# Two matrix products in the bilinear form: sums on one engine, joined and in pairs, in new orders

## The chip, the cores and the metric

The kernel runs on one core of a Trainium2 chip. The metric is device time in microseconds (us) of one execution. The engines are TensorE (PE, matrix products into the eight banks of PSUM; PEld is its weight load), VectorE (DVE), ScalarE (ACT), GpSimd (POOL), and SyncE (SP, which here only issues DMAs). Each engine works through its own instructions in order and waits for the others by semaphores.

## The reference, cut to what matters

```python
batch, m, k, h, n = 16, 512, 768, 3072, 768
y = np.matmul(x, w1) + b1          # x: 8192 rows of 768 in all, w1: 768 x 3072
y = np.maximum(y, 0)
return np.matmul(y, w2)            # w2: 3072 x 768
```

Inputs and result are float32. The kernel multiplies in float16 and collects sums of squares of its inputs (`stat`), by which a flag at the end chooses a general path, which is not taken here.

## The kernel before

**Blocks.** The hidden axis of 3072 is done in two halves (`c` = 0, 1), the 8192 rows in eight blocks of 1024 (`MB`). That makes 16 blocks of work, `it` = 0 to 15; blocks 0 to 7 are the first half, 8 to 15 the second. Block 8 has the rows of block 7 again, so x stays where it is across the switch, and new w1 and w2 are loaded there. The results of the second half are added in DRAM to those of the first by accumulating DMAs from GpSimd's queue; only the last block reads the earlier result back and adds it on the core (`add_priors`, `add_prior`).

**Stages.** A block has two stages, each a matrix product in a bilinear form of the kind of Strassen's, with 20 products of sub-blocks in place of 24. In the first stage (`add_first`, L878) x is a 4 x 2 grid of sub-blocks and w1 a 2 x 3 grid, for each of two groups of columns: 40 products of six matmuls (256 columns each), L896. In the second (`add_second`, L995) y is a 4 x 3 grid, w2 a 3 x 2 grid: 20 products of eight matmuls (384 columns each), L1016. Block 0's first stage is a plain product instead (L802).

**Sums.** A product multiplies a sum of x sub-blocks by a sum of w1 sub-blocks. `X_SUMS`, `Y_SUMS`, `W1_SUMS` and `W2_SUMS` list them as (output, input, input, sign): numbers below 8 for x (12 for y, 6 for w) are the sub-blocks as loaded, higher ones are sums. `FIRST_U`, `FIRST_V`, `SECOND_U` and `SECOND_V` say which sum a product takes. `place` (L202) gives each its slot; slots of dead sub-blocks are used again. A block needs 16 sums of x (L640, 768 elements a partition, five of them on GpSimd by `X_POOL`) and 16 of y (L869). A y sum covers both column groups (1024 elements) where `Y_JOIN` names it; the others are done for each group (512), six of these twelve on GpSimd by `Y_POOL`. The y sums of a block can be made when its first stage has given the y sub-blocks; the x sums of the next block when its x has been loaded (GpSimd's queue, L565) and transposed by eight DMAs on SP (L619). The sums of w1 (L657, for each group) and w2 (L679) are made in block 0 and at the switch, where the planner may put each on VectorE or GpSimd.

**Chains.** Products add up in PSUM along chains. `SECOND_CHAINS` lists them: ('m', p) is product p, ('t', t) is operation t of `SECOND_OPS`, which reads the chain's two banks and writes an output (`out`, to one of four buffers `o` and from there to DRAM), a kept sum (`sum`, in `s`) or the starting value of another chain (`seed`, into PSUM). An operation with a kept sum as second operand runs on VectorE (L1031), one without on ScalarE (L1028). A chain of the second stage holds two banks, one of the first stage one. `SECOND_ORDER` and `FIRST_ORDER` are the orders of TensorE's products; `SWITCH_ORDER` is that of blocks 7 and 8, `LAST_ORDER` that of block 15.

**The planner.** `Graph.run` is a list scheduler: each task has an engine, a cost in ns written in the code (a y sum of 1024: 685, one of 512: 426, on GpSimd 1180; an x sum: 552, on GpSimd 1650), a due time and an allowance for crossing to another engine (`CROSS`). TensorE's order is fixed; the planner sets the order on the other engines and gives out banks, kept-sum places and output buffers. The instructions are issued in that order. Its squares (`idle` tasks) fill gaps of ScalarE.

## Time and profile before

| what | value |
|---|---|
| median of 3 runs | 1073.01 us (1070.94 to 1074.68) |
| the profiled execution | 1072.51 us, span 1070.9 us |
| granted TensorE clock, mean | 0.951 |
| DMA | 115.15 MB, mean 108 GB/s |
| block 4: first stage, second stage | 26.20 us, 38.51 us |
| starts of the first stages, blocks 1, 7, 9, 15 | 78.36, 469.50, 615.26, 1002.59 us |

The lines below are of the profiled execution, in us from its span's start. A line of the timeline has start, length, engine, line of the kernel, operation, output<-input with shapes, count, and in brackets the idle time before it and what ended that. A line of the groups has count | busy us, mean ns of one | idle time before them and what ended most of it. A line of the windows has the stretch, its length, the busy time and count of each engine named in its header, TensorE's granted clock, the busy share of the DMA engines, and GB/s. For one source line, min/median/max of an instruction are given.

### The profile page before, as it was taken

To read this page: it belongs to the slowest core of one execution; us is meant where nothing else is said; L and a number is where in the kernel's file an instruction comes from. 1 tells how busy PE (TensorE), PEld (TensorE's weight loads), DVE (VectorE), ACT (ScalarE), POOL (GpSimd) and SP (SyncE) were. 2 spreads that over 40 slices of the span, in tenths; PEclk is the share of its full clock that TensorE was granted. 3 is DMA by queue.
4 is the path that set the end of the run, shared out by engine and by line. 5 is a ranking of instruction groups with operands and counts; after the bars stand their busy time and mean duration, and the time that the engine had idled before them with its cause. 6 is when DMAs were issued, how large, how long until landed. Compare 5 with 4: busy or idle time off the path is not lost. (4 is left out here: it accounts for less than half of the span.)

```text
span 1070.9 us, 16568 instructions
## 1 busy us (share of the span) xinstructions
PE 905.8 (85%) x6445; PEld 644.0 (60%) x6445; DVE 831.7 (78%) x1060; ACT 472.9 (44%) x919; POOL 440.5 (41%) x333
## 2 busy tenths in 40 slices
PE   9889798896978969788688896986979889797986
PEld 8458376483755738466356483763847658484763
DVE  4888959679696886958976879586796978869694
ACT  7737557563461725525324173463523415152340
POOL 6521605216052250615652617244272552716353
PEclk9999899898999999899889899999999999899998
DMA  9963283852638345183315572855738586461833
GB/s 210 174 160 73 47 188 52 172 109 53 169 52 185 60 97 133 45 184 107 115 74 89 80 123 40 143 89 89 109 53 142 81 135 103 68 111 30 120 117 119
DMA packets 159717, 115.15 MB, mean 108 GB/s; under 512 B 93052, under 2 KB 158100, under 8 KB 159380
## 3 DMA queue, kind: packets, MB, share of 16 engines
q0 software_dynamic: 46496, 54.27, 32.6%
q1 hardware_dynamic: 112672, 58.81, 22.4%
q8 instruction: 51, 0.84, 0.3%
q10 hardware_dynamic: 468, 1.00, 0.2%
q14 instruction: 30, 0.25, 0.1%
HBM read 73.94 MB, written 55.05 MB: 120 GB/s over the span
## 5 line engine op out<-in xcount | busy, mean ns | idle before, releaser
L1016 PE MATMUL ps<-v,y 128*128 128x384 f16 x2560 | 468.9, 344 | 142.8 <-DVE o L1031 51.9
L1016 PEld LDWEIGHTS <-y 128*128 128x128 f16 x2560 | 260.9, 102 | 347.2 <-issue 179.8
L896 PE MATMUL ps<-x,v 128*128 128x256 f16 x3600 | 399.9, 274 | 12.9 <-DVE s L936 4.3
L896 PEld LDWEIGHTS <-v 128*128 128x128 f16 x3600 | 353.6, 98 | 58.8 <-issue 15.7
L869 DVE TENSOR_TENSOR y<-y 128x1024 f16<-128x1024 f16 (+1 forms) x266 | 272.2, 1065 | 12.9 <-POOL y L869 9.7
L869 POOL TENSOR_TENSOR y<-y 128x512 f16<-128x512 f16 x96 | 134.9, 1422 | 341.5 <-ACT y L930 230.5
L933 DVE CUSTOM_DVE_ANT_0 y<-ps,s 128x512 f16<-128x512 f32 x240 | 161.9, 688 | 92.3 <-PE ps L896 54.5
L640 POOL TENSOR_TENSOR x<-x 128x768 f16<-128x768 f16 x70 | 133.7, 1918 | 85.3 <-DVE x L640 60.1
L1028 ACT ACTIVATE ps<-ps 128x768 f32<-128x768 f32 x80 | 63.6, 795 | 232.4 <-PE ps L1016 138.8
L930 ACT ACTIVATE s<-ps,bt 128x256 f32<-128x256 f32 x180 | 74.0, 471 | 180.8 <-PE ps L896 164.7
L640 DVE TENSOR_TENSOR x<-x 128x768 f16<-128x768 f16 x154 | 123.3, 847 | 2.1 <-DMA x<-xn 2.0
L1060 POOL DMA_DIRECT2D out_dram<-o x56 | 67.3, 1245 | 64.1 <-DVE o L1031 62.8
L930 ACT ACTIVATE y<-ps,bt 128x256 f16<-128x256 f32 x180 | 73.3, 471 | 29.2 <-PE ps L896 27.8
L1028 ACT ACTIVATE s<-ps 128x768 f32<-128x768 f32 x64 | 51.7, 808 | 75.3 <-PE ps L1016 73.2
L1031 DVE TENSOR_TENSOR o<-ps,s 128x768 f32<-128x768 f32 x60 | 57.1, 952 | 29.5 <-ACT ps L1028 19.8
L1031 DVE TENSOR_TENSOR o<-s,ps 128x768 f32<-128x768 f32 x60 | 56.6, 949 | 25.0 <-PE ps L1016 11.7
L565 POOL DMA_DIRECT2D xn<-in_x_dram x30 | 23.4, 782 | 97.7 <-DVE y L933 65.4
L627 ACT ACTIVATE xn<-xn 128x768 f16<-128x768 f16 x60 | 50.1, 839 | 1.6 <-DMA x<-xn 1.6
L926 ACT ACTIVATE ps<-ps 128x512 f32<-128x512 f32 x60 | 34.7, 582 | 24.1 <-DVE y L933 15.8
L930 ACT ACTIVATE ps<-ps,bt 128x256 f32<-128x256 f32 x60 | 26.9, 448 | 17.2 <-PE ps L896 11.5
L802 PE MATMUL ps<-x,v 128*128 128x256 f16 (+1 forms) x216 | 31.9, 308 | 0.8 <-DMA v<-in_w_dram 0.5
L679 DVE TENSOR_TENSOR v<-v 128x768 f16<-128x768 f16 x36 | 27.8, 808 | 3.9 <-DMA v<-in_w_dram 3.9
(65 smaller groups left out, 407.0 us busy)
## 6 DMA issues: line engine op xcount, KB each, us to landing
out_dram<-o SPq DMA_DIRECT2D x71, 384.0 KB, 6.2
xn<-in_x_dram POOLq DMA_DIRECT2D x28, 768.0 KB, 7.9
out_dram<-o POOLq DMA_DIRECT2D x56, 384.0 KB, 6.8
x<-out_dram SPq DMA_DIRECT2D x8, 384.0 KB, 3.4
v<-in_w_dram POOLq DMA_DIRECT2D x6, 384.0 KB, 8.8
v<-in_w_dram POOLq DMA_DIRECT2D x12, 192.0 KB, 10.1
w1d<-in_w_dram POOLq DMA_DIRECT2D x6, 384.0 KB, 17.2
w2d<-in_w_dram POOLq DMA_DIRECT2D x12, 192.0 KB, 15.1
```

What stands on the lines that cost most here:

```text
L627: self.nc.scalar.activation(out=self.xn[:, s, :], in_=self.xn[:, s, :], func=ACTF.Square, accum_out=self.stat[:, self.stat_at["x"] + i:][: ...
L640: e.tensor_tensor(out=x[:, a], in0=x[:, b], in1=x[:, c], op=ALU.add if sign > 0 else ALU.subtract)
L802: nc.tensor.matmul(self.ps[:, ps.at[0], cols], lhsT=self.v1[:, gi, 2 * h + k2, k, j * P:(j + 1) * P], rhs=rhs, start=(k2 == 0 and k == 0), ...
L869: e.tensor_tensor(out=self.y[:, a, cols], in0=self.y[:, b, cols], in1=self.y[:, c, cols], op=ALU.add if sign > 0 else ALU.subtract)
L896: nc.tensor.matmul(self.ps[:, at, j * self.QM:(j + 1) * self.QM], lhsT=self.v1[:, gi, self.w1s[FIRST_V[p]], k, j * P:(j + 1) * P], rhs=sel ...
L926: nc.scalar.activation(out=out, in_=ps, scale=float(a), func=func if kind == "out" else ACTF.Copy)
L930: nc.scalar.activation(out=out[:, halves[j]], in_=ps[:, halves[j]], func=func, scale=float(a), bias=beta(j))
L933: nc.vector._custom_dve(TENSOR_ADD_SAT, out=out, in0=ps, in1=s, s0=F_MAX, s1=0.0)
L1016: nc.tensor.matmul(self.ps[:, bank[ch].at[j], 0:NH], lhsT=self.y[:, self.ys[SECOND_U[p]], m0:m0 + P], rhs=self.v2[:, slot[SECOND_V[p]], s, :],
L1028: nc.scalar.activation(out=out, in_=ps, func=ACTF.Copy, scale=float(a))
L1031: engine.tensor_tensor(out=out, in0=in0, in1=in1, op=ALU.add if a == b else ALU.subtract)
L1060: nc.gpsimd.dma_start(out=rows, in_=out, accum_op=ALU.add)
```

## The change

All sums go to VectorE; GpSimd keeps its DMAs and the adds of the last block. A y sum always covers both column groups (1024 elements), except in block 0, and a w1 sum covers both groups (2 x 768). Where `X_FUSE` or `Y_FUSE` names a sum, it and the next one of the table become one operation over two slots each (`two`): as one run where the slots lie side by side, as two rows where not. A block has 10 + 3 operations for its x sums and 12 + 2 for its y sums. The tables of sums, the bilinear form of the second stage (seven chains in place of eight) and the orders of products in both stages are new; the order of blocks 7 and 8 is that of the others. In blocks 0 and 7 (`APART`) an output that has a kept sum as second operand leaves in two parts: SP stores the kept sum, ScalarE copies the banks to an output buffer, and GpSimd's accumulating DMA adds that in DRAM. The squares write to a tile of their own (`junk`) instead of an output buffer, in halves for w2, and are spread over more blocks (`STATS`). The planner's allowance from TensorE to others is 0.15 instead of 0.22 us, and tasks with a choice of two engines are gone.

```diff
-FIRST_ORDER = (16, 0, 36, 4, 12, 28, 8, 7, 18, 24, 9, 1, 15, 38, 21, 10, 3, 14, 35, 30, 6, 11, 32,
-    17, 37, 34, 5, 27, 31, 29, 2, 26, 22, 19, 25, 33, 20, 23, 39, 13)
-SWITCH_ORDER = (16, 4, 8, 0, 18, 15, 1, 10, 12, 14, 6, 17, 11, 7, 13, 9, 5, 2, 3, 19, 36, 24, 32,
-    28, 38, 29, 27, 35, 21, 30, 23, 34, 37, 31, 26, 20, 25, 22, 33, 39)
...
-Y_SUMS = ((13, 3, 4, 1), (18, 0, 13, 1), (14, 2, 8, 1), (15, 11, 5, 1), (12, 9, 10, 1), (27, 8, 7,
-    1), (19, 7, 14, 1), (16, 6, 12, 1), (20, 1, 19, 1), (17, 10, 15, 1), (21, 17, 3, -1), (23, 15,
-    16, 1), (22, 21, 0, -1), (25, 18, 20, 1), (26, 11, 10, 1), (24, 14, 16, -1))
-SECOND_U = (1, 19, 6, 4, 22, 12, 27, 0, 23, 13, 5, 16, 18, 7, 24, 26, 25, 2, 17, 10)
...
+FIRST_ORDER = (36, 4, 16, 20, 12, 0, 8, 7, 9, 18, 24, 28, 10, 1, 15, 3, 21, 38, 32, 14, 35, 29,
+    27, 30, 11, 34, 23, 26, 37, 31, 6, 5, 17, 25, 2, 22, 13, 33, 39, 19)
+SWITCH_ORDER = (36, 4, 16, 20, 12, 0, 8, 7, 9, 18, 24, 28, 10, 1, 15, 3, 21, 38, 32, 14, 35, 29,
...
+Y_SUMS = ((16, 3, 0, 1), (21, 5, 3, 1), (15, 8, 7, 1), (12, 11, 10, 1), (19, 5, 16, 1), (18, 1,
+    15, 1), (20, 2, 19, 1), (14, 6, 9, -1), (17, 11, 14, -1), (22, 1, 17, 1), (26, 18, 20, 1),
+    (24, 7, 22, 1), (13, 4, 12, -1), (23, 11, 9, 1), (27, 13, 14, 1), (25, 13, 16, -1))
+SECOND_U = (6, 2, 8, 26, 5, 21, 17, 23, 27, 19, 13, 4, 25, 12, 15, 11, 24, 18, 0, 1)
+SECOND_V = (0, 5, 7, 17, 9, 0, 10, 3, 16, 11, 14, 1, 13, 4, 1, 8, 12, 15, 3, 4)
...
 SECOND_OPS = {
...
+    0: (0, 1, 11, 1, 'out', 4, None),
+    1: (2, 1, 9, 1, 'out', 5, None),
+    2: (1, 1, 11, 1, 'out', 6, None),
+    3: (2, 1, None, None, 'out', 7, None),
+    4: (1, 1, 8, 1, 'out', 2, None),
+    5: (3, -1, 8, 1, 'out', 3, None),
+    6: (0, -1, 9, 1, 'out', 0, None),
+    7: (3, 1, None, None, 'out', 1, None),
+    8: (1, -1, 13, 1, 'sum', None, None),
+    9: (0, 1, 10, 1, 'sum', None, None),
+    10: (4, 1, 16, -1, 'sum', None, None),
+    11: (5, 1, None, None, 'sum', None, None),
+    12: (5, -1, None, None, 'seed', 0, None),
+    13: (6, 1, None, None, 'sum', None, None),
+    14: (5, 1, 16, 1, 'seed', 2, None),
+    15: (1, -1, None, None, 'seed', 5, None),
+    16: (1, 1, None, None, 'sum', None, None),
+    17: (3, -1, 19, 1, 'seed', 1, None),
+    18: (4, -1, None, None, 'seed', 3, None),
+    19: (6, 1, None, None, 'sum', None, None),
...
-SECOND_ORDER = (11, 17, 19, 1, 15, 5, 18, 13, 6, 14, 3, 2, 10, 12, 9, 0, 7, 16, 8, 4)
...
-X_POOL = (0, 2, 4, 12, 14)
-Y_POOL = ((0, 4), (0, 8), (0, 9), (0, 11), (1, 2), (1, 8))
-Y_JOIN = (0, 3, 5, 6, 7, 10, 12, 13, 14, 15)
+SECOND_CHAINS = ((('m', 2), ('t', 9), ('m', 14), ('t', 0), ('m', 3), ('t', 6)), (('m', 9), ('t',
+    16), ('m', 13), ('t', 15), ('m', 10), ('t', 8), ('m', 11), ('t', 4), ('m', 8), ('t', 2)),
+    (('m', 7), ('t', 3), ('m', 16), ('t', 1)), (('m', 1), ('t', 17), ('m', 18), ('t', 7), ('m',
+    12), ('t', 5)), (('m', 19), ('t', 18), ('m', 17), ('t', 10)), (('m', 15), ('t', 14), ('m', 6),
+    ('t', 12), ('m', 0), ('t', 11)), (('m', 5), ('t', 19), ('m', 4), ('t', 13)))
+SECOND_SEEDS = (12, 17, 14, 18, None, 15, None)
+SECOND_ORDER = (19, 5, 1, 4, 9, 17, 13, 18, 15, 10, 12, 6, 7, 11, 2, 0, 14, 8, 16, 3)
...
+X_FUSE = (3, 8, 11)
+Y_FUSE = (2, 13)
...
-    CROSS = {"PE": 0.22, "DVE": 0.08, "ACT": 0.08, "POOL": 0.1, "SP": 0.1}
+    CROSS = {"PE": 0.15, "DVE": 0.08, "ACT": 0.08, "POOL": 0.1, "SP": 0.1}
...
+APART = (0, 7)
+
+STATS = ((1, 2, 3, 4, 5, 6, 7), (2, 3, 4))
...
+    def sums_of(self, table, slots, fused):
+
+        n, out = 0, []
+        while n < len(table):
+            m = 2 if n in fused else 1
+            rows = [[slots[v] for v in table[n + k][:3]] for k in range(m)]
+            sign = table[n][3]
+            if m == 2:
+                rows = self.ordered(*rows, sign)
+            out.append((*(tuple(v) for v in zip(*rows)), sign))
+            n += m
+        return out
+
...
+    @staticmethod
+    def two(view, at):
+
+        if len(at) == 1:
+            return view[:, at[0]]
+        a, b = at
+        if a == b:
+            return view[:, a:a + 1].to_broadcast([P, 2, view.shape[2]])
+        return view[:, a:b + 1:b - a]
...
+        for out, in0, in1, sign in self.sums_of(X_SUMS, self.xs, X_FUSE):
+            def add(out=out, in0=in0, in1=in1, sign=sign):
                 x = self.x.rearrange("p a k m -> p a (k m)")
-                e.tensor_tensor(out=x[:, a], in0=x[:, b], in1=x[:, c],
-                                op=ALU.add if sign > 0 else ALU.subtract)
-            self.g.add(engine, 1650 if engine == "POOL" else 552, add,
-                       reads=[("x", q, h) for q in (b, c) for h in range(2)],
-                       writes=[("x", a, h) for h in range(2)])
+                self.nc.vector.tensor_tensor(
+                    out=self.two(x, out), in0=self.two(x, in0), in1=self.two(x, in1),
+                    op=ALU.add if sign > 0 else ALU.subtract)
+            self.g.add("DVE", 552 if len(out) == 1 else 950, add,
+                       reads=[("x", q, h) for q in in0 + in1 for h in range(2)],
+                       writes=[("x", a, h) for a in out for h in range(2)])
...
+    def add_w1_sums(self):
+
+        for o, i, j, sign in W1_SUMS:
             a, b, d = (self.w1s[q] for q in (o, i, j))
 
+            def add(a=a, b=b, d=d, sign=sign):
+                w = self.v1.rearrange("p g a k h -> p g a (k h)")
+                self.nc.vector.tensor_tensor(out=w[:, :, a], in0=w[:, :, b], in1=w[:, :, d],
+                                             op=ALU.add if sign > 0 else ALU.subtract)
+            self.g.add("DVE", 950, add,
+                       reads=[("w1", g, q) for g in range(2) for q in (b, d)],
+                       writes=[("w1", g, a) for g in range(2)])
...
-                self.g.add(engine, 685 if both else 1180 if engine == "POOL" else 426, add,
-                           reads=[k for q in (b, c) for h in gs for k in self.y_keys(q, h)],
-                           writes=[k for h in gs for k in self.y_keys(a, h)])
+    def add_y_sums(self, groups=(0, 1)):
+
+        n = len(groups)
+        cols = slice(512 * groups[0], 512 * groups[-1] + 512)
+        for out, in0, in1, sign in self.sums_of(Y_SUMS, self.ys, Y_FUSE if n == 2 else ()):
+            def add(out=out, in0=in0, in1=in1, sign=sign):
+                y = self.y[:, :, cols]
+                self.nc.vector.tensor_tensor(
+                    out=self.two(y, out), in0=self.two(y, in0), in1=self.two(y, in1),
+                    op=ALU.add if sign > 0 else ALU.subtract)
+            self.g.add("DVE", 426 if n == 1 else 685 if len(out) == 1 else 1217, add,
...
-                combine(nc.scalar if u is None else nc.vector, out, ps, a,
-                        None if u is None else sum_of(kept[u]), b)
-
-        def store(to, reg):
+                alone = u is None or (kind == "out" and apart)
+                combine(nc.scalar if alone else nc.vector, out, ps, a,
+                        None if alone else sum_of(kept[u]), b)
+
+        def store(to, reg, plain):
             out, rows = self.o[:, reg.at[0]].rearrange("p (a n) -> p a n", a=2), \
                 self.rows_of(it, to)
-            if c == 0 or final:
+            if plain:
                 nc.sync.dma_start(out=rows, in_=out)
             else:
                 nc.gpsimd.dma_start(out=rows, in_=out, accum_op=ALU.add)
+
+        def store_sum(to, u):
+            (nc.gpsimd if c else nc.sync).dma_start(
+                out=self.rows_of(it, to), in_=sum_of(kept[u]),
+                **({"accum_op": ALU.add} if c else {}))
...
+                elif u is not None and apart:
+                    assert b == 1
+                    self.g.add("POOL" if c else "SP", 1375 if c else 100,
+                               lambda to=to, u=u: store_sum(to, u), reads=[kept[u]],
+                               writes=[("out", self.block(it), to)], lat=6.5)
+                    engine = "ACT"
...
-                plain = c == 0 or final
+                plain = c == 0 and (u is None or not apart) or final
```

197 lines of the change are left out of this document (72 added, 125 removed), and 4 rows, old and new, of the table SECOND_CHAINS.

## The prediction, made before the result was known

> **What bounds the kernel now.** I read the busy shares first, then one block by stages, then the timelines of TensorE, VectorE and GpSimd over the same stage.
>
> ```profile
> PE 905.8 (85%) x6445; PEld 644.0 (60%) x6445; DVE 831.7 (78%) x1060; ACT 472.9 (44%) x919; POOL 440.5 (41%) x333
> ...
> core 0: us, PE busy (x) PEld busy (x) DVE busy (x) ACT busy (x) POOL busy (x), PEclk, DMA share, GB/s
> 340.36:366.56 26.20, 26.20 (x242) 23.49 (x241) 17.80 (x29) 16.73 (x39) 1.42 (x1) 1.00 0.45 113
> 366.56:405.07 38.51, 28.66 (x163) 16.09 (x161) 32.79 (x34) 11.82 (x21) 20.37 (x15) 0.96 0.50 103
> ```
>
> The first stage of a block is pure TensorE, 26.2 us at a clock of 1.00. The second takes 38.5, and VectorE is busy for 32.8 of it.
>
> ```profile
> 366.56 4.06 PE L1016 MATMUL ps<-v,y 128*128 128x384 f16 x24
> 371.12 1.47 PE L1016 MATMUL ps<-v,y 128*128 128x384 f16 x8 [0.50 <-DVE y L869]
> 373.54 6.66 PE L1016 MATMUL ps<-v,y 128*128 128x384 f16 x40 [0.94 <-ACT ps L1028]
> 384.95 5.74 PE L1016 MATMUL ps<-v,y 128*128 128x384 f16 x24 [4.76 <-ACT ps L1028]
> 392.42 4.06 PE L1016 MATMUL ps<-v,y 128*128 128x384 f16 x24 [1.72 <-DVE ps L1031]
> 397.36 2.76 PE L1016 MATMUL ps<-v,y 128*128 128x384 f16 x16 [0.88 <-ACT ps L1028]
> 401.17 4.06 PE L1016 MATMUL ps<-v,y 128*128 128x384 f16 x24 [1.05 <-DVE s L1031]
> ```
>
> Forty matmuls take 6.66 and eight 1.47, so 32 take 5.19: 0.162 each, 1.30 a product of eight, 26.0 for the 20 products. The other 12.5 us are the gaps in brackets (9.85), 1.68 of slow matmuls after the long gap (24 take 5.74, not 4.06), and some 0.17 of pipeline end at each gap. Why VectorE is late:
>
> ```profile
> 360.93 0.69 DVE L869 TENSOR_TENSOR y<-y 128x1024 f16<-128x1024 f16 x1
> 362.14 0.41 DVE L869 TENSOR_TENSOR y<-y 128x512 f16<-128x512 f16 x1
> 377.52 4.12 POOL L640 TENSOR_TENSOR x<-x 128x768 f16<-128x768 f16 x2
> 378.14 2.01 DVE L869 TENSOR_TENSOR y<-y 128x1024 f16<-128x1024 f16 x1
> 384.60 1.82 POOL L640 TENSOR_TENSOR x<-x 128x768 f16<-128x768 f16 x1 [2.96 <-DVE x L640]
> 384.85 1.99 DVE L640 TENSOR_TENSOR x<-x 128x768 f16<-128x768 f16 x1
> 389.69 1.56 POOL L565 DMA_DIRECT2D xn<-in_x_dram  x2
> 390.94 0.54 DVE L640 TENSOR_TENSOR x<-x 128x768 f16<-128x768 f16 x1
> ...
> 366.56:405.07 38.51, 15.41 (x12) 7.07 (x5) 0.96 0.50 103
> ...
> 366.56:405.07 38.51, 8.33 (x11) 9.86 (x5) 0.96 0.50 103
> ```
>
> A sum of 1024 takes 0.69 alone and 2.01 beside a GpSimd sum; one of 768 takes 0.54 beside a GpSimd DMA issue and 1.99 when it starts inside a GpSimd sum: it ends 0.4 after that sum. The last two rows are the window for the y line and the x line alone (VectorE, then GpSimd). Twelve y sums took 15.41; eight of 1024 and four of 512 at the free price are 7.2. Eleven x sums took 8.33, free 6.0. So 10.5 us a block are lost on VectorE to GpSimd's sums, nearly TensorE's idle time.
>
> **The change, part by part.** Prices:
>
> ```profile
> L869 DVE TENSOR_TENSOR y<-y 128x1024 f16<-128x1024 f16 x150 | 184.3, 1251 | 8.0 <-POOL y L869 5.2
> L640 DVE TENSOR_TENSOR x<-x 128x768 f16<-128x768 f16 x154 | 123.3, 847 | 2.1 <-DMA x<-xn 2.0
> L1063 POOL TENSOR_TENSOR x<-x,s 128x768 f32<-128x768 f32 x8 | 15.5, 1962 | 10.1 <-DVE s L1031 10.1
> L1031 DVE TENSOR_TENSOR o<-ps,s 128x768 f32<-128x768 f32 x60 | 57.1, 952 | 29.5 <-ACT ps L1028 19.8 <-PE ps L1016 4.9 <-DMA out_dram<-o 2.8
> L1028 ACT ACTIVATE ps<-ps 128x768 f32<-128x768 f32 x80 | 63.6, 795 | 232.4 <-PE ps L1016 138.8 <-DVE s L1031 55.7 <-DVE o L1031 22.1
> L619 SPq DMA_TRANSPOSE x<-xn x112: 1210/1275/3133, 40.3 to 966.8; - x112
> ...
> DMA to landing us min/median/max: 2.7/2.8/8.0
> ```
>
> *Sums.* No row shows a sum of two neighbours. From 512 to 1024 costs 0.28, so 2048 costs about 1.25 and 1536 about 0.97. A block's y sums become 12 at 0.69 and two at 1.25, 10.8; its x sums 10 at 0.54 and three at 0.97, 8.3. The rest of VectorE's block is 24.7: the two windows hold 17.80+32.79 = 50.6, less the second stage's sums (15.41+8.33) and the first stage's four y sums (two of 0.69, two of 0.41). Together 43.8, under TensorE's 26.2+26.0 = 52.2, although VectorE takes over all that GpSimd did (mean 1251 and 847 ns of VectorE's own sums fall to 690 and 540). The two-row form could instead run at half speed: one y and one x sum a block would grow by 1.12 and 0.84, each joined w1 sum by 0.84. I take full speed, as the rows are whole contiguous runs like those measured, and keep the other as a rival. The Trainium skill ("Vector Engine (DVE) Microarchitecture Reference", section 5.1, Performance modes) asks 16-bit operands and an innermost step of one for the fast mode, which two rows meet; no run here shows it yet. By that page the sum stands; without it the half-speed rival below would hold.
>
> *Orders.* I walked one steady block with the rows' times, 0.2 from the end of a product to its reader. A product can start when the operation before it in its chain has read or seeded its banks and its y sum is there; VectorE and ACT take their operations in the order in which the planner put them. Second stage, first product (19) at 0, one more each 1.30, as SECOND_ORDER has them. Product 1 is third, due at 2.60; its seed t18 reads product 19 on ACT behind the first stage's last output, 1.6 to 2.4: in time. Product 9, due at 5.20, needs t17, which waits for product 1 (3.9) and has VectorE from 4.1 to 5.05. Product 6, due at 14.3, needs t14: product 15 ends at 11.7, VectorE is free at 12.2, done 13.15. Product 11, due at 16.9, needs t8: 13.2 to 14.1. Product 14, due at 20.80, needs t9, done 20.80 to 20.85. Product 3, due at 24.75, needs t0: 22.3 to 23.3. Between them run the y sums (their order is the diff's): the fused pair 15 and 12 from 1.9 to 3.1, needed from 7.8; ten of the twelve behind the first stage are done by 9.0, the last two (20 and 26, needed at 24.75) by 11.3; then x sums between the outputs, to 21.9. So nothing waits over 0.1 us, and every product has another one between it and its seed; in the old order some follow their seed at once (the gaps of 0.88 to 1.05). The first stage walks through likewise, with 0.3 us to spare at the tightest (t0, before product 14). I charge 1.0 us a block for what a walk misses; the bounds are 0 and the three quoted gaps of about 1 plus one more, 3.8.
>
> *Transposes.* Three single x sums and one pair move into the first stage, on VectorE, behind six DMA transposes on SP. A first-stage product is 26.2/40 = 0.656; the raw places are last read by the 26th and the 30th product, free 17.1 and 19.7 us into the stage; at 1.3 each the sixth goes out at 21.0 and lands at 23.8, VectorE gets there at 24.2. This cover is thin: a landing of 8.0 instead of 2.8 makes VectorE 4.8 late, with the last two outputs and the y sums queued behind, of which products 1 and 9 have 1.3 to spare. At the median it costs 0.
>
> *GpSimd and SP.* GpSimd keeps x loads and accumulating stores; its queue only gets emptier, and loads go out earlier. Output buffers: four, each held until its store lands.
>
> ```profile
> L1060 POOL DMA_DIRECT2D out_dram<-o x56: 1179/1197/1651, 603.1 to 1006.2; - x56
> ...
> L1058 SPq DMA_DIRECT2D out_dram<-o x71: 372/372/414, 59.9 to 1064.2; - x71
> ```
>
> In blocks 0 and 7, six outputs go to ACT (0.80, it is busy 11.8 of 38.5) instead of VectorE (0.95), with six plain stores on SP (0.37) and six accumulating ones on GpSimd (1.2) more, 12 transfers of 384 KB in all. Each accumulating store waits on GpSimd for its plain store's landing, with the next x and w loads queued behind it, of which the first is needed a block later; nothing of TensorE waits for them, but the kept sums hold their places until their store lands. A gain is there too: six times 0.95 off VectorE. Between a loss of 6 us (one landing) and that gain, per block; I take the gain into VectorE's sums below and 1 us of loss into the two items below. The rearranged squares stay on ACT: 0.
>
> ```profile
> 19.87 22.91 PE L802 MATMUL ps<-x,v 128*128 128x256 f16 x138 [0.35 <-DVE x L752]
> 45.34 2.93 PE L1016 MATMUL ps<-v,y 128*128 128x384 f16 x16 [2.57 <-DVE v L679]
> 78.36 26.36 PE L896 MATMUL ps<-x,v 128*128 128x256 f16 x240 [0.61 <-DVE o L1031]
> 469.50 2.78 PE L896 MATMUL ps<-x,v 128*128 128x256 f16 x24
> 615.26 26.56 PE L896 MATMUL ps<-x,v 128*128 128x256 f16 x240
> 1002.59 26.36 PE L896 MATMUL ps<-x,v 128*128 128x256 f16 x240
> 1028.79 11.86 PE L1016 MATMUL ps<-v,y 128*128 128x384 f16 x72
> 1062.37 2.75 DVE L1031 TENSOR_TENSOR o<-x,ps 128x768 f32<-128x768 f32 x4
> ```
>
> *The sum.* Twelve steady blocks (1 to 6, 9 to 14) took (469.50-78.36)+(1002.59-615.26) = 778.5; now 12 x (52.2+1.0) = 638.4. Blocks 7 and 8 took 145.8; VectorE gets two blocks of 43.8 less 8.3 (no x sums between, the same rows follow), less 5.7 (outputs on ACT), plus 12 w1 sums of 0.97 and 24 w2 sums of 0.54 (22 of all these were GpSimd's), 98 of 104.4. The new order of block 8 draws on both groups of w1 from the start, so all 12 w1 sums must be done with block 7: 11.6, 8.7 of y sums and five operations of 0.95 are 25.1 of its 26.0. Tight, so I take 2 us lost in each block, 108.4; the bounds are 0 and the 10 us that the w1 sums would be late if their loads came last. Block 0 ended at 78.36. Its opening run ends at 42.8 and the second stage began at 45.34 behind a w2 sum; its first two products now need two plain w2 blocks and y sums of that moment, 43.3, it lasts 26.0, and I give 3.7 for the sums of w that trail into block 1: 73. The bounds are 69.3 and 78.4. The last block took 68.3. Its second stage, walked with six GpSimd adds of 1.96, the last four in a row from 22.4, has VectorE done after 31.3 instead of 1062.37+2.75-1028.79 = 36.3: 63.2. Span 73+638.4+108.4+63.2 = 883. The profiled execution was 1072.5 for a span of 1070.9, 0.5 under the median of 1073.0: 883+1.6+0.5 = 885.
>
> **Rivals.** *Half-hidden chains:* three or four gaps of about 1 us stay in each second stage, since they come from product-to-seed latency and not from sums. For: the rows 0.94, 0.88, 1.05. Against: the new order puts a product between. 14 blocks x 2.8 more: 924. *Transfers:* the same bytes in 0.83 of the time raise the DMA share from about 0.5 to 0.6 and more; landings near the maxima (8.0) hold the transposes or the four output buffers, 2 us a block: 913. *Half-speed pairs:* 2 us of VectorE in each of 14 blocks, half of it seen since VectorE has 8 us to spare, and 12 x 0.84 = 10 us in each of two runs of w1 sums, 18 of 20 seen: 917. *The other side:* the inflated sums are VectorE's own price, from something that stays. Then y sums cost 12 x 1.25 and two of 2.5, 20.0, x sums 13.6 at the mean 0.85, and VectorE 58.3 a block; with the 14.1 us that it waits now (64.7 less 50.6) a block is 72.4, 7.7 more, and 14 of them give 1181. It decides from 25.9 us of sums a block (VectorE back at 50.6), against 19.1 free. Against it: 0.54 beside a DMA issue, 1.99 beside a sum, 3 us apart. *No effect:* VectorE gets free and TensorE waits as before; the rows name VectorE in front of the long gaps, so I hold it small.
>
> **How the numbers follow.** Forecast 0.60 (885, own range 868 to 906), chains 0.14, transfers 0.14, half-speed 0.05, other side 0.06, no effect 0.01. A change under 0.3%, about 3 us, could not be told from none. Faster is all but the last two, 0.93; same 0.01; slower 0.06. The lower end is TensorE's own work, 42.8 to the end of its opening run, 15 x 26.2, 16 x 26.0 and about 7 at the end, 859, with the last block's adds, 866; the upper end takes in chains and transfers together with a margin, 942.
>
> **What would show it.** Right: no GpSimd TENSOR_TENSOR in y or x until the last block; the mean of a 1024 sum near 0.69 (was 1.25); second stages of 26 to 28 us; PEclk near 1.00 throughout; TensorE above 95%. Chains wrong: gaps of 0.9 behind ACT ps. Transposes wrong: VectorE waiting for x<-xn at each block's end. Pairs wrong: 2 x 1024 well above 1.25. The prediction falls if second stages stay above 32 us.

## The result, and the profile after

| | time, us |
|---|---|
| before, median of 4 | 1071.97 (1070.88 to 1074.68) |
| changed, median of 4 | 941.41 (939.94 to 942.75) |
| ratio | 0.8778, 95% interval 0.8755 to 0.8802 |
| forecast | 885, range 866 to 942 |

The kernel is 131 us faster; 188 were forecast. The time lies inside the range by 0.6 us, at its upper end, and above the forecast's own range (868 to 906). The profiled execution took 942.75 for a span of 941.1. The first fence is from the page of the changed kernel: engines, and groups as count | busy, mean ns | idle before.

```profile
PE 865.2 (92%) x6445; PEld 631.1 (67%) x6445; DVE 690.3 (73%) x1052; ACT 477.8 (51%) x951; POOL 142.9 (15%) x155
...
L1032 PE MATMUL ps<-v,y 128*128 128x384 f16 x2560 | 430.9, 326 | 56.6 <-ACT ps L1044 18.9
L911 PE MATMUL ps<-x,v 128*128 128x256 f16 x3600 | 398.6, 273 | 9.4 <-DVE o L1047 2.6
```

The second stage's matmuls in the kernel before:

```profile
L1016 PE MATMUL ps<-v,y 128*128 128x384 f16 x2560 | 468.9, 344 | 142.8 <-DVE o L1031 51.9 <-ACT ps L1028 42.3 <-DVE ps L1031 19.5
```

The span fell by 129.8 us. TensorE's idle time gave 89.2 of them (165.1 to 75.9) and its busy time 40.6 (905.8 to 865.2): a matmul of the second stage takes 326 ns instead of 344 in the mean, at a granted clock of 0.998 instead of 0.951.

And these are the changed kernel's sums, each shape by itself:

```profile
L884 DVE TENSOR_TENSOR y<-y 128x1024 f16<-128x1024 f16 x180 | 123.0, 687 | 2.9
L661 DVE TENSOR_TENSOR x<-x 128x768 f16<-128x768 f16 x140 | 74.9, 551 | 14.8 <-DMA x<-xn 14.3
L661 DVE TENSOR_TENSOR x<-x 128x1536 f16<-128x1536 f16 x42 | 40.0, 953 | 0.5
L884 DVE TENSOR_TENSOR y<-y 128x2048 f16<-128x2048 f16 x30 | 36.5, 1217 | 0.0
```

VectorE's prices are those of the forecast, and VectorE is at 73%. What is missing is in one place: 56.6 us in which TensorE waits inside the second stage (L1032). The next fence has the windows of blocks 4 and 8, each with its first and its second stage.

```profile
core 0: us, PE busy (x) PEld busy (x) DVE busy (x) ACT busy (x) POOL busy (x), PEclk, DMA share, GB/s
249.97:276.17 26.20, 26.20 (x242) 23.46 (x240) 20.18 (x33) 20.82 (x49) 0.00 (x0) 1.00 0.34 85
276.17:308.84 32.67, 27.23 (x162) 15.59 (x160) 22.03 (x30) 12.62 (x23) 3.54 (x5) 1.00 0.69 145
482.06:510.31 28.25, 26.52 (x243) 23.44 (x241) 24.88 (x46) 15.62 (x35) 5.63 (x5) 1.00 0.72 132
510.31:536.63 26.32, 26.31 (x162) 15.63 (x160) 24.72 (x35) 7.78 (x11) 7.96 (x7) 1.00 0.94 136
```

Block 4's second stage takes 32.67 us with VectorE busy for 22.0 of it; block 8's takes 26.32 with VectorE busier, 24.7. (The stages of 26.20 and 38.51 us in the table of the kernel before, from 340.36 to 405.07, are those of its block 5; its block 4 starts at 275.77 and takes 26.20 and 38.39.) TensorE's timeline in both:

```profile
276.17 9.26 PE L1032 MATMUL ps<-v,y 128*128 128x384 f16 x56
286.13 1.46 PE L1032 MATMUL ps<-v,y 128*128 128x384 f16 x8 [0.70 <-DVE s L1047]
288.54 5.86 PE L1032 MATMUL ps<-v,y 128*128 128x384 f16 x33 [0.94 <-ACT ps L1044]
295.31 1.30 PE L1032 MATMUL ps<-v,y 128*128 128x384 f16 x7 [0.92 <-DVE o L1047]
297.50 4.06 PE L1032 MATMUL ps<-v,y 128*128 128x384 f16 x24 [0.88 <-ACT ps L1044]
302.70 2.92 PE L1032 MATMUL ps<-v,y 128*128 128x384 f16 x17 [1.15 <-DVE s L1047]
306.41 2.60 PE L1032 MATMUL ps<-v,y 128*128 128x384 f16 x15 [0.78 <-DVE o L1047]
...
510.31 26.49 PE L1032 MATMUL ps<-v,y 128*128 128x384 f16 x160
```

The same twenty products in the same order stop six times in block 4 and not once in block 8. So the order of products alone does not make the gaps. The operations that bear on the first two gaps of block 4 are, line by line, t17, t10, product 18, t15, and product 15 with those after it:

```profile
280.35 0.96 DVE L1047 TENSOR_TENSOR ps<-s,ps 128x768 f32<-128x768 f32 x1 [0.66 <-PE ps L1032]
285.13 0.95 DVE L1047 TENSOR_TENSOR s<-ps,s 128x768 f32<-128x768 f32 x1
286.13 1.46 PE L1032 MATMUL ps<-v,y 128*128 128x384 f16 x8 [0.70 <-DVE s L1047]
287.69 0.80 ACT L1044 ACTIVATE ps<-ps 128x768 f32<-128x768 f32 x1 [2.36 <-PE ps L1032]
288.54 5.86 PE L1032 MATMUL ps<-v,y 128*128 128x384 f16 x33 [0.94 <-ACT ps L1044]
```

Read them with `SECOND_ORDER` and `SECOND_CHAINS` beside. Fifty-six matmuls are seven products, so what starts at 286.13 is the eighth, product 18. It continues chain 3, whose last operation, t17, ended at 280.35 + 0.96 = 281.31. Yet it starts when t10 ends (285.13 + 0.95 = 286.08), an operation of chain 4, with which it shares no bank. Likewise t15 on ScalarE reads chain 1 after product 13, which ended at 276.17 + 9.26 = 285.43; it starts at 287.69, when product 18 is over (286.13 + 1.46 = 287.59). The planner's list of banks has chain 4 in banks 2 and 4, chain 3 in 3 and 6, chain 1 in 5 and 7. Bank 3 lies between 2 and 4, bank 6 between 5 and 7. An operation reads its two banks as one strided operand (`pair`: `self.ps[:, a:b + 1:b - a, 0:NH]`).

### The profile page after: what moved, and what is told of

It reads as the page before. It is cut to its first block, busy times and chain, and to the rows that moved or that the text cites. A ratio compares the mean times of both kernels' runs of the same rounds, so it can differ in the third digit from the quotient of the medians.

```text
span 941.1 us, 16251 instructions
## 1 busy us (share of the span) xinstructions
PE 865.2 (92%) x6445; PEld 631.1 (67%) x6445; DVE 690.3 (73%) x1052; ACT 477.8 (51%) x951; POOL 142.9 (15%) x155
## 4 chain that ended last, share of the span: by engine, by line
PE 73%; DVE 10%; DMA 6%; issue 4%; ACT 4%; POOL 1%; SPq 0%; DVEq 0%; POOLq 0%; ACTq 0%
PE ps L911 39%; PE ps L1032 31%; DVE o L1047 3%; PE ps L821 3%; DVE y L884 3%; DMA x<-xn 2%; DVE s L1047 2%; DMA out_dram<-o 2%; ACT ps L1044 2%; DVE x L661 1%; DMA out_dram<-s 1%; ACT o L1044 1%; DMA v<-in_w_dram 1%; ACT xn L620 1%; DVE ps L1047 1%
## 5 line engine op out<-in xcount | busy, mean ns | idle before, releaser
L1032 PE MATMUL ps<-v,y 128*128 128x384 f16 x2560 | 430.9, 326 | 56.6 <-ACT ps L1044 18.9
L1032 PEld LDWEIGHTS <-y 128*128 128x128 f16 x2560 | 249.7, 98 | 233.6 <-issue 74.1
L884 DVE TENSOR_TENSOR y<-y 128x1024 f16<-128x1024 f16 (+2 forms) x242 | 170.2, 718 | 8.5 <-ACT y L830 5.2
L661 DVE TENSOR_TENSOR x<-x 128x768 f16<-128x768 f16 (+1 forms) x182 | 112.8, 644 | 15.3 <-DMA x<-xn 14.3
L1077 POOL DMA_DIRECT2D out_dram<-o x68 | 81.6, 1282 | 213.9 <-DMA out_dram<-s 74.3
L1044 ACT ACTIVATE ps<-ps 128x768 f32<-128x768 f32 x48 | 38.2, 795 | 147.3 <-PE ps L1032 105.9
L1044 ACT ACTIVATE o<-ps 128x768 f32<-128x768 f32 x42 | 33.7, 808 | 11.2 <-PE ps L1032 6.4
L1047 DVE TENSOR_TENSOR s<-ps,s 128x768 f32<-128x768 f32 x32 | 30.5, 953 | 8.0 <-PE ps L1032 8.0
L945 ACT ACTIVATE ps<-ps,bt 128x256 f32<-128x256 f32 x60 | 26.8, 447 | 14.1 <-PE ps L911 10.9
L1047 DVE TENSOR_TENSOR o<-s,ps 128x768 f32<-128x768 f32 x26 | 24.6, 948 | 6.4 <-DMA out_dram<-o 2.3
L1047 DVE TENSOR_TENSOR ps<-ps,s 128x768 f32<-128x768 f32 x16 | 15.5, 966 | 18.8 <-ACT o L1044 10.5
```

The source lines that it names most:

```text
L661: self.nc.vector.tensor_tensor(out=self.two(x, out), in0=self.two(x, in0), in1=self.two(x, in1), op=ALU.add if sign > 0 else ALU.subtract)
L884: self.nc.vector.tensor_tensor(out=self.two(y, out), in0=self.two(y, in0), in1=self.two(y, in1), op=ALU.add if sign > 0 else ALU.subtract)
L945: nc.scalar.activation(out=out[:, halves[j]], in_=ps[:, halves[j]], func=func, scale=float(a), bias=beta(j))
L1032: nc.tensor.matmul(self.ps[:, bank[ch].at[j], 0:NH], lhsT=self.y[:, self.ys[SECOND_U[p]], m0:m0 + P], rhs=self.v2[:, slot[SECOND_V[p]], s, :],
L1044: nc.scalar.activation(out=out, in_=ps, func=ACTF.Copy, scale=float(a))
L1047: engine.tensor_tensor(out=out, in0=in0, in1=in1, op=ALU.add if a == b else ALU.subtract)
```

## Experiments

**Theory A:** an operation whose two banks are not neighbours waits, and makes others wait, as if it used every bank from the first to the second. **Theory B:** VectorE comes late, since sums of y stand ahead of t10 in its queue, and the order leaves no slack. The twelve runs answer three questions. All ratios are to the kernel before, run beside them on the same chip (1070.6 to 1071.1 us).

### Do the bank numbers make the gaps?

Three kernels have the instructions of the changed kernel in the same order on every engine; they differ in bank numbers alone. The first renames banks after the planning:

```diff
         self.order = sorted(order, key=lambda t: (t.start, t.n))
+        for r in {r for t in self.tasks for r in t.regs if r.kind == "ps"}:
+            r.at = sorted((0, 1, 2, 4, 3, 6, 5, 7)[i] for i in r.at)
```

> The changed kernel with every instruction on every engine in the same order and of the same shape; only the eight PSUM banks are renamed (3 and 4 change places, 5 becomes 6, 6 becomes 5). In blocks 2 to 6 the four bank pairs of the second stage, which were 2+4, 0+1, 3+6 and 5+7, become 2+3, 0+1, 4+5 and 6+7; block 1 goes from 3+4, 0+1, 2+6, 5+7 to 3+4, 0+1, 2+5, 6+7 (the form that blocks 8 and 9 had); blocks 7, 8 and 9 get the pairs 4+6 or 2+6 and 5+7, which reach into one another. Theory A (an operation on a pair of banks that are not neighbours waits, and makes others wait, as if it took every bank from its first to its second, so that chains which share no bank wait for one another): second stages of blocks 2 to 6 fall from 32.6-33.6 us to 26.2-27.3, block 1 from 32.0 to about 26.5, while those of blocks 8 and 9 rise from 26.3 and 26.8 to 30 or 31 and block 7 from 27.5 to about 31; the whole 941 - 37 + 12 = 916, between 908 and 926. Theory B (VectorE's queue is late: the sums of y stand ahead of the kept sum that the next chain needs, and the written order leaves no slack): the order is the same, so 941 within 3 us, and the same gaps in the same blocks.

Measured: 924.04 (923.27 to 925.7), ratio 0.863, interval 0.8613 to 0.8646. The second gives out neighbours, in `Graph.take`:

```diff
+            if reg.n == 2:
+                at = {i: (f, full) for f, full, i in found}
+                found = sorted((max(at[i][0], at[i + 1][0]), at[i][1] + at[i + 1][1], i)
+                               for i in range(0, 8, 2) if i in at and i + 1 in at)
+                if not found or found[0][0] > 1e8:
+                    return None
+                return found[0][0], [found[0][2], found[0][2] + 1]
```

> The changed kernel with the same order on every engine, but each pair of banks of the second stage is two neighbours (0+1, 2+3, 4+5, 6+7) in every block. Theory A: TensorE's gaps of 0.7 to 1.2 us in the second stages go in all blocks; by the table of the second stages (32.0, 32.6 three times, 33.6 twice, 30.6 to 30.8 four times, 29.7, each less 26.4) some 57 us, 941 - 57 = 884, between 876 and 895. Theory B: 941 within 3 us.

Measured: 879.77 (877.76 to 879.9), ratio 0.8206, interval 0.8189 to 0.8222. The third takes these neighbours apart again, with (0, 2, 1, 3, 4, 6, 5, 7) as the renaming.

> The kernel with neighbouring pairs, its order kept, with banks 1 and 2 and banks 5 and 6 renamed into one another, so that in every block the pairs are 0+2, 1+3, 4+6 and 5+7: two and two of them reach into one another. Theory A: gaps of about 0.9 us behind operations of other chains in every second stage, blocks 8 and 9 among them, 2 to 6 us a block: 884 + 16 x 4 = 948, between 915 and 980. Theory B: the time of the kernel with neighbouring pairs, whatever that is, within 3 us.

Measured: 991.44 (988.8 to 992.18), ratio 0.9248, interval 0.9227 to 0.927. The length of the second stages, from the start of its first matmul to that of the next stage, in us:

| block | pairs as changed | changed | renamed | neighbours | crossed |
|---|---|---|---|---|---|
| 1 | 3+4, 0+1, 2+6, 5+7 | 32.0 | 26.0 | 26.0 | 33.6 |
| 2 to 4 | 2+4, 0+1, 3+6, 5+7 | 32.6 to 32.7 | 26.0 | 26.0 | 33.6 |
| 5, 6 | the same | 33.6, 33.6 | 26.9, 26.4 | 27.0, 26.9 | 34.2, 34.0 |
| 7 | 2+4, 0+1, 3+5, 6+7 | 27.5 | 28.5 | 26.0 | 36.2 |
| 8, 9 | 3+4, 0+1, 2+5, 6+7 | 26.3, 26.8 | 31.4, 32.6 | 26.0, 26.7 | 33.6, 34.0 |
| 10 | 3+4, 0+1, 5+6, 2+7 | 30.6 | 30.6 | 26.0 | 29.8 |
| 14 | 0+4, 1+2, 3+5, 6+7 | 29.7 | 31.5 | 26.4 | 33.6 |

The renaming turns the four pairs of block 10 into themselves, and its stage keeps its length. In blocks 8 and 9 of the changed kernel the pair 2+5 reaches over 3+4 and costs nothing: there chain 4 has banks 3 and 4, so t10 reaches over no bank of chain 3, and product 18 does not wait for it. So by theory A a pair that reaches over another costs time only where work on the banks between falls due meanwhile.

TensorE's timeline of the renamed kernel, block 4 and block 8:

```profile
264.86 26.16 PE L1034 MATMUL ps<-v,y 128*128 128x384 f16 x160
...
480.39 10.56 PE L1034 MATMUL ps<-v,y 128*128 128x384 f16 x64
491.89 5.36 PE L1034 MATMUL ps<-v,y 128*128 128x384 f16 x32 [0.94 <-ACT ps L1046]
497.98 1.46 PE L1034 MATMUL ps<-v,y 128*128 128x384 f16 x8 [0.73 <-DVE o L1049]
500.33 4.06 PE L1034 MATMUL ps<-v,y 128*128 128x384 f16 x24 [0.88 <-ACT ps L1046]
505.52 2.76 PE L1034 MATMUL ps<-v,y 128*128 128x384 f16 x16 [1.14 <-DVE s L1049]
509.23 2.76 PE L1034 MATMUL ps<-v,y 128*128 128x384 f16 x16 [0.94 <-DVE o L1049]
```

With no instruction moved in any engine's order, the gaps left block 4 and came to block 8. And the operations around t15 in block 4 of the renamed kernel:

```profile
273.82 0.95 DVE L1049 TENSOR_TENSOR s<-ps,s 128x768 f32<-128x768 f32 x1
274.22 0.80 ACT L1046 ACTIVATE ps<-ps 128x768 f32<-128x768 f32 x1 [0.20 <-PE ps L1034]
```

t10 starts as long after the stage's start as before (273.82 - 264.86 = 8.96; 285.13 - 276.17 = 8.96): VectorE is just as late. But t15 now starts 9.36 after it, not 11.52. Theory B falls. The renamed kernel is 8 us above the 916 expected, mostly because block 0, which the expectation left out, went from 26.5 to 33.7 us with its new pairs. The crossed kernel lost more than expected, about 6.5 us of gaps in most blocks against 4.

Is it the range of one operand, or something in the chip about neighbouring banks? Three kernels write each operation as two, one for each bank:

```diff
-                combine(nc.scalar if alone else nc.vector, out, ps, a,
-                        None if alone else sum_of(kept[u]), b)
+                for j in range(2):
+                    combine(nc.scalar if alone else nc.vector, out[:, j], ps[:, j], a,
+                            None if alone else sum_of(kept[u])[:, j], b)
```

On the crossed banks:

> The kernel with crossed bank pairs (0+2, 1+3, 4+6, 5+7; 991 us, gaps of 6.5 us in most second stages), its order kept, but each operation of the second stage written as two instructions, one for each bank of the pair, on the same engine one after the other. Theory A in its strict form (what waits is the range of addresses of one instruction's operand, from its first bank to its last): an instruction on one bank has no bank between, so the gaps behind other chains go, and what is left is the price of the second instruction in each chain, some 0.2 to 0.4 us for each operation on TensorE's path where the chain has no slack: 880 to 915. If crossed pairs are slow for a reason of the chip (two engines in neighbouring banks at one time): near 991, or above it.

Measured: 877.02 (875.89 to 877.72), ratio 0.8189, interval 0.8175 to 0.8203: the gaps go, and the second instructions cost less than expected. On the changed kernel's own banks:

> The changed kernel with its own bank pairs (2+4, 0+1, 3+6, 5+7 in blocks 2 to 6) and its order, each operation of the second stage written as two instructions, one for each bank of the pair. Theory A (a range of addresses from the first bank to the last): the gaps go without any change of banks, 875 to 885. If the bank numbers themselves matter: 941.

Measured: 874.2 (872.99 to 875.24), ratio 0.8166, interval 0.8149 to 0.8184. On neighbours:

> Neighbouring bank pairs, and each operation of the second stage as two instructions of one bank. Theory A: with the ranges of neighbouring banks nothing is left for the split to free, so it is like neighbouring pairs alone (880) or like crossed pairs split (877): 874 to 884. If a product can start on the first bank while the second is still being written, the chains' latency falls by half an operation and some of the gaps of 0.2 to 0.7 us go: the lower end.

Measured: 875.12 (873.86 to 876.23), ratio 0.8173, interval 0.8154 to 0.8193. TensorE's second stage on the pages of four kernels: crossed, crossed and split, changed and split, neighbours.

```profile
L1041 PE MATMUL ps<-v,y 128*128 128x384 f16 x2560 | 439.6, 327 | 96.1 <-DVE ps L1056 33.0
```
```profile
L1041 PE MATMUL ps<-v,y 128*128 128x384 f16 x2560 | 420.2, 326 | 3.7 <-ACT ps L1053 2.5
```
```profile
L1032 PE MATMUL ps<-v,y 128*128 128x384 f16 x2560 | 421.5, 327 | 4.1 <-DVE o L1047 2.0
```
```profile
PE 853.1 (97%) x6445; PEld 631.5 (72%) x6445; DVE 691.1 (79%) x1052; ACT 478.4 (54%) x951; POOL 142.8 (16%) x155
...
L1039 PE MATMUL ps<-v,y 128*128 128x384 f16 x2560 | 420.5, 326 | 4.7 <-ACT ps L1051 3.1
L918 PE MATMUL ps<-x,v 128*128 128x256 f16 x3600 | 397.4, 273 | 10.8 <-DVE o L1054 4.2
```

With the worst pairs and the same banks, splitting takes 96.1 us of waits down to 3.7. So engines at work in banks beside each other cost nothing that shows; what costs is one operand that reaches over other chains' banks. The waits stand in the program: in the trace of the changed kernel the last matmul of product 13 carries a signal for the other engines (it raises a semaphore) in block 8 and none in block 4, where the next signal is that of product 18, for which t15 then waits. The split costs little: ScalarE's seeds become 0.47 and VectorE's operations 0.55 for each half (0.80 and 0.95 whole), and VectorE is busy 699.5 us instead of 691.1, which TensorE does not feel. The changed kernel with split operations is 67 us under the changed kernel and 18% under the kernel before; the three split kernels (874.2 to 877.0) are hardly told apart.

### What is each part of the change worth?

```diff
-X_POOL = (0, 2, 4, 12, 14)
-Y_POOL = ((0, 4), (0, 8), (0, 9), (0, 11), (1, 2), (1, 8))
-Y_JOIN = (0, 3, 5, 6, 7, 10, 12, 13, 14, 15)
+X_POOL = ()
+Y_POOL = ()
+Y_JOIN = tuple(range(16))
```

This, in the kernel before, with the sums of w kept from GpSimd too:

> The kernel before with its own orders of products and its bank pairs, with one part of the change: no sum of x, y or the weights on GpSimd, all sums of y joining both groups. No pair sums, no outputs in two parts. Theory of the prediction (the two-input sums on GpSimd slow VectorE's): a 1024-wide sum of y falls from 1.4 us and more to 0.69, the gaps of 1.5 to 5.4 us that wait for VectorE in the second stages go, some 5.5 to 6.5 us a block in 13 blocks: 1072 - 78 = 994, between 980 and 1012; its gaps of 0.88 to 1.05 in blocks 2 to 6 stay, since the bank pair 0+7 there reaches over all others. Rival (VectorE is late for the work that it gets in place of GpSimd, 5 sums of x and 6 of y): little or nothing gained, 1050 or more.

Measured: 940.95 (939.09 to 942.8), ratio 0.8777, interval 0.876 to 0.8793: this part alone gives what the whole change gives, and 53 us more than the 994 expected of it. TensorE's block 3 of it:

```profile
223.00 5.36 PE L1016 MATMUL ps<-v,y 128*128 128x384 f16 x32
229.30 6.66 PE L1016 MATMUL ps<-v,y 128*128 128x384 f16 x40 [0.94 <-ACT ps L1028]
236.90 4.06 PE L1016 MATMUL ps<-v,y 128*128 128x384 f16 x24 [0.93 <-ACT ps L1028]
242.07 4.06 PE L1016 MATMUL ps<-v,y 128*128 128x384 f16 x24 [1.11 <-DVE ps L1031]
247.01 2.76 PE L1016 MATMUL ps<-v,y 128*128 128x384 f16 x16 [0.88 <-ACT ps L1028]
250.82 4.06 PE L1016 MATMUL ps<-v,y 128*128 128x384 f16 x24 [1.05 <-DVE s L1031]
```

The gaps of 0.94, 0.88 and 1.05 are those that the prediction quoted of the kernel before. There the pair 0+7 reaches over all others. Then the neighbouring pairs (the edit shown above) in the kernel before, and in this one:

> The kernel before, its order kept on every engine and its sums left on GpSimd, with one edit: pairs of neighbouring banks. Its pairs in blocks 1 to 6, 9 to 11 and 13 to 15 reach into or over one another (1+2, 3+4, 5+6 and 0+7 in blocks 2 to 6); in blocks 7, 8 and 12 they are neighbours already. Theory A: the gaps of 0.88 to 1.11 us in blocks 1 to 6 go (3.8 to 4.7 us a block with their restarts), and some 2 us in each of the later ones, while the gaps behind VectorE (3.85 to 5.4 and 1.67) stay and may grow into the freed time: 1071 - 6 x 3.5 - 6 x 2 = 1038, between 1022 and 1055. If the bank pairs cost something only in the new orders of products: 1071 within 4 us.

Measured: 1049.62 (1046.75 to 1050.76), ratio 0.9797, interval 0.9776 to 0.9818: 21 us, fewer than the 33 expected. The gaps of 0.88 to 1.05 went; the gap behind VectorE stayed (4.92 in block 6, where it was 4.75).

> The old orders of products, no sums on GpSimd, all sums of y in both groups, neighbouring bank pairs: neither the new orders nor pair sums nor outputs in two parts. Its counterpart with the old pairs took 941 us, with second stages of 31.7 to 34.5 us in blocks 0 to 6, 31.7 in blocks 9 and 10. Theory A: those fall to 26 to 27.7; 7.5 + 5 + 5 x 5 + 2 x 5 + some 4 in blocks 11 to 15, 941 - 52 = 889, between 880 and 900. If the new orders are worth something by themselves, the changed kernel with neighbouring pairs (880) is faster than this one by what they are worth; by the prediction's count of the chains (3.8 us a block before) it would be up to 45 us, by theory A less than 10.

Measured: 879.93 (877.87 to 880.07), ratio 0.8218, interval 0.8204 to 0.8231. Side by side:

| | own pairs | neighbouring pairs |
|---|---|---|
| before | 1071 | 1049.6 |
| before, no sums on GpSimd, all y sums joined | 940.95 | 879.93 |
| the whole change | 941.41 | 879.77 |

Rows two and three are equal in both columns. The new orders, the pair sums, the two-part outputs and all else that is new are together worth nothing that these runs can measure. What joining the sums of y is worth by itself no run shows. The bank pairs cost 21 us while VectorE held TensorE up anyway, and 61 once it did not.

Two parts were also taken away alone, from the kernel with neighbouring pairs (879.77): pair sums (`X_FUSE = Y_FUSE = ()`) and outputs in two parts (`APART = ()`).

> The changed kernel with neighbouring bank pairs, without pair sums: every sum of x and y is an instruction of its own. VectorE has 3 x (2 x 0.551 - 0.953) + 2 x (2 x 0.687 - 1.217) = 0.76 us more a block, and it is busy 79% of the span: hidden, so 880 within 4 us. If a pair sum makes other instructions wait for the rows that lie between its two (x 7 and 19, y 9 and 19), as a pair of banks does for the banks between, then without pair sums the gaps that are left (0.45 to 1.9 us in first stages) would shrink: 870 to 876.

Measured: 884.9 (884.59 to 885.3), ratio 0.8264, interval 0.825 to 0.8278. It is 5.1 us slower, but not where the expectation looked: VectorE's busy time is 692.6 us against 691.1, hardly more. Block 1's first stage takes 39.5 us, not 31.3; all the rest is 3.4 us shorter. The planner's order changed with the edit, so what block 1 lost to, order or sums, stays open. The gaps in the other first stages stayed, so rows that lie apart show no price of the size that banks have; a small one is not excluded, since the second stages of blocks 5, 6 and 9 fell from 27.0, 26.9 and 26.7 to 26.1, 26.0 and 26.0. Why a pair saves so little shows in the changed kernel's timeline of VectorE:

```profile
57.57 0.55 DVE L699 TENSOR_TENSOR v<-v 128x768 f16<-128x768 f16 x1
58.03 0.42 DVE L884 TENSOR_TENSOR y<-y 128x512 f16<-128x512 f16 x1
...
60.04 0.95 DVE L661 TENSOR_TENSOR x<-x 128x1536 f16<-128x1536 f16 x1
60.91 0.95 DVE L677 TENSOR_TENSOR v<-v 128x1536 f16<-128x1536 f16 x1
```

The second sum starts 0.09 before the first one's row ends, and the fourth 0.08 before the third one's. A sum of 768 so costs its queue 0.46, two cost 0.92, and a pair 0.87: it saves 0.05, where the rows (0.55 twice against 0.95) promise 0.15. The Trainium skill ("Perfetto Trace Analysis", section "Optimizing Scalar/DVE Operations") says that the part of an instruction's profiled latency in which its writes are acknowledged overlaps with the next instruction. These rows agree, with an overlap of 0.08 to 0.09.

> The changed kernel with neighbouring bank pairs, without outputs in two parts: blocks 0 and 7 make their outputs like the others. The prediction put the two parts at a loss of 1 us in each of the two blocks: 878, between 874 and 881. If they take work off VectorE where it is late (block 7 has gaps in the stage after it): slower, 882 to 888.

Measured: 880.2 (879.7 to 880.62), ratio 0.8219, interval 0.8202 to 0.8237: no difference that could be told from none.

### Does a sum on GpSimd make VectorE's dearer by itself?

The run without GpSimd's sums takes two things away: the load beside VectorE, and GpSimd's slow links in the chains of sums. This one puts only the load back:

```diff
+    def add_idle_sum(self, reads):
+        self.g.add("POOL", 650, lambda: self.nc.gpsimd.tensor_tensor(
+            out=self.z, in0=self.z, in1=self.z, op=ALU.add), reads=reads, writes=["z"])
```

> The kernel with neighbouring bank pairs with all its sums on VectorE, and beside them sums on GpSimd that nobody uses: 27 of 256 wide in a block (as much width as the 11 sums of a block that GpSimd made before), of a small tile of zeros with itself, ready when the rows are that GpSimd's sums once read. No instruction waits for their result. The prediction's term (a two-input sum on GpSimd makes VectorE's two-input sums dearer while it runs, 10.5 us a block): VectorE's mean 1024 sum rises from 0.69 to some 1.0 or more, its work in a block from 43.8 to about 54 us against TensorE's 52.2, and the time from 880 to 940, between 905 and 985. If the 130 us came from taking slow links out of the chains of sums (GpSimd's 2.0 us where VectorE needs 0.55) and not from a price that it puts on VectorE: 880 within 5.

Measured: 905.98 (903.86 to 907.24), ratio 0.8464, interval 0.8443 to 0.8484: 26 us slower than without the load, at the lower end of what was expected of a price. Three groups of sums of this kernel:

```profile
L679 POOL TENSOR_TENSOR z<-z 128x256 f16<-128x256 f16 x390 | 309.9, 795 | 27.6 <-POOL z L679 0.4
L898 DVE TENSOR_TENSOR y<-y 128x1024 f16<-128x1024 f16 x180 | 129.6, 724 | 2.9
L668 DVE TENSOR_TENSOR x<-x 128x768 f16<-128x768 f16 x140 | 93.9, 687 | 19.3 <-DMA x<-xn 18.8
```

The price is there without any data passing between the two: a sum of 768 rises from 551 to 687 ns in the mean, one of 1024 from 687 to 724, and VectorE is busy for 728.6 us, not 691.1. But it is 2.5 us a block, not 10.5. Few of VectorE's sums of 1024 met one of GpSimd's: counted in the trace, 28 of 180 touched one, and the 17 that such sums covered for nine tenths or more took 941 ns. In the kernel before 92 of 150 touched one, the 60 so covered took 1596, and the 58 that touched none took 685. VectorE's operations with one input in PSUM show no such price: 49 of the 52 outputs o<-ps,s touched a sum on GpSimd and took 953 ns, where the kernel without the load has 957.

The 26 us are not the price alone. Block 1's second stage takes 34.1 us instead of 26.0, because VectorE waits 7.06 us there for a transpose (x<-xn), and the planner's order on VectorE and ScalarE changed in places.

How large the price was in the kernel before, its own rows show: VectorE's 494 sums of two float16 inputs took 198 us more than at the means of those that touched no sum on GpSimd (685 ns for 1024 elements, 547 for 768, 414 for 512). Without GpSimd's sums VectorE was busy 709.3 us instead of 831.7, although it took over their 188 sums. So the mechanism is shown, and what it cost VectorE; its share in the 131 us is not, because the slow links in the chains went at the same time, and the sums of this run were shorter than GpSimd's old ones. The Trainium skill ("SBUF — State Buffer", section "SBUF: two separate sides") says that VectorE's operations with two inputs in SBUF and GpSimd's operations that read SBUF hold a shared pair of ports by turns, each for a whole instruction. The rows agree in direction, and in sparing the operations with an input in PSUM; how long each of the two waited for the other they do not tell.

## Why the prediction was right, and which step was wrong

The kernel got faster once GpSimd's sums were gone, as the prediction said, but by 57 us less than forecast. That the time still lies in the range is luck. Its upper end was set for half-hidden chains and busy transfers, and what filled it was a cost of some 61 us that the prediction did not have. (The prediction says that 942 takes in both with a margin; they add 39 and 28 us to 885, which makes 952.) By its own sign the prediction falls, since the second stages of blocks 1 to 6 take 32.0 to 33.6 us; and TensorE is busy for 92% of the span, not over 95. The sum's items against the trace of the changed kernel and of the one with neighbouring pairs, us:

| item | forecast | changed | neighbours |
|---|---|---|---|
| block 0 to its end | 73 | 69.5 | 69.2 |
| twelve steady blocks | 638.4 | 700.1 | 641.1 |
| blocks 7 and 8 | 108.4 | 108.2 | 106.5 |
| block 15 | 63.2 | 63.2 | 61.5 |
| span | 883 | 941.1 | 878.2 |

- **VectorE's prices: right.** Forecast 0.69, 0.54, 1.25 and 0.97; measured 0.687, 0.551, 1.217 and 0.953. Half-speed pairs fall. So does the other side (the inflated sums as VectorE's own price, 1181). VectorE's block was put at 43.8; block 4's windows hold 20.18 + 22.03 = 42.2.
- **The orders: wrong, and nearly all of the miss.** The walk found no wait over 0.1 us and charged 1.0 a block, at most 3.8. Block 4's six gaps are 5.4 us, and its stage is 32.67, not 26 or 27. The walk let a product start when the operation before it in its own chain was done and the sum was there. That holds where the operands keep to their banks: block 4's stage takes 26.0 us in the kernel with neighbouring pairs and in all three with split operations, with the same order of products. What it lacked was a third condition, an operation on another chain whose operand reaches over this chain's bank. The code's `pair` and the planner's bank numbers were at hand, and so was a sign in the trace of before: gaps of 0.88 to 1.05 in blocks 1 to 6, and only the long VectorE gaps (4.75, 3.79 and 4.52) in blocks 7 and 8, whose pairs were neighbours.
- **Half-hidden chains (924): the sign without the cause.** Its sign appeared, gaps of 0.9 behind ACT ps. As a latency from product to seed it is refuted, since with the same order and other bank numbers the gaps are gone. The prediction took the gaps of before for such a latency, too.
- **GpSimd's load on VectorE: mechanism right, size not separated.** Removing GpSimd's sums gives the whole gain (940.95), in a run that also joins all sums of y. The price on VectorE is shown; what share of the gain comes from it and what from shorter chains is open.
- **Transposes: nearly as costed.** VectorE waits 14.3 us for x<-xn in all, in twelve waits of 1.2 in the mean. With neighbouring pairs it waits 13.0; where the wait is longest in a steady block (1.8 to 2.1 us, blocks 5, 6 and 9) the second stage takes 0.7 to 1.0 us more than 26.0, behind VectorE's late y.
- **Transfers (913): small.** With neighbouring pairs and 136 GB/s, TensorE's first stages wait 10.8 us in all, 4.2 of that behind outputs on VectorE. Outputs on VectorE in turn wait 8.2 us for stores out of the output buffers, so the rival's mechanism is there, at a fraction of its 28 us.
- **Two-part outputs: the gain is there, the loss does not show.** VectorE is busy 691.1 us with them and 701.0 without. Of the loss of 1 us in each of two blocks nothing is seen: 879.8 us with them, 880.2 without.
- **Pair sums: their worth was overrated.** Each row was priced right, but the next instruction starts before a row ends, so a pair of 768 saves 0.05 us and not 0.15.

## What to carry to other kernels

When an operand takes two banks, or two of anything, with a step between them, look at what lies between: here a chain there had to wait where its work fell due at the same time, and neighbouring places or one instruction for each place took the waits away. A gap that recurs with the same length in some blocks and is absent in others with the same order of work is no latency of that order; compare what differs, down to the numbers of the banks. And before many parts of a change are priced together, the cheapest of them deserves a run alone: here three settings, with the sums of w kept from GpSimd too, gave all of the gain.

## What the runs showed of the hardware that was not expected

- Splitting an operation on 768 elements in two costs little: ScalarE's seed 0.80 becomes two of 0.47, VectorE's sum 0.95 two of 0.55, and the kernel becomes no slower (ratios 0.8189, 0.8173 and 0.8166 against 0.8206 unsplit with neighbouring pairs; only the last lies outside its interval).
- A VectorE sum's row overlaps the next one's by 0.08 to 0.09 us, so sums of 768 follow one another every 0.47 us (the median in the changed kernel's trace), and joining two in one instruction saves little: VectorE is busy 691.1 us with pairs, 692.6 without.
- A sum on GpSimd that shares no data with VectorE's raised VectorE's sums beside it from 687 to 941 ns (1024 elements), and left operations with one input in PSUM at 953 ns (957 without it).
